# A two-layer diffusion backbone on one core: the partial-product stage put into a forced order of loads, with three modulation chunks moved

## The chip, the cores and the metric

The kernel runs on one core of one Trainium2 chip. The metric is the device time of one execution in microseconds (us). The engines are named as in the profile: PE (TensorE), PEld (its weight loads), DVE (VectorE), ACT (ScalarE), POOL (GpSimd) and SP (SyncE, which issues the DMA transfers here). L227 is line 227 of the kernel.

## What is computed

256 latent and 256 context tokens of width 2048 pass through two layers, all in fp32. Each layer has a token mixer (layer 0: pooling in four channel groups, layer 1: neighbourhood attention) and a gated MLP of width 5504 with a width-3 convolution. Shift, scale and gate of each sub-layer are made from the condition:

```
silu_c, silu_cc = jax.nn.silu(c), jax.nn.silu(c_ctx)
for i in range(DEPTH):
    ml = (silu_c @ w_mod[i] + b_mod[i]).reshape(B, 6, 1, D)
    mc = (silu_cc @ w_mod[i] + b_mod[i]).reshape(6, 1, 1, D)
    a_lat = modulate(rms_norm(h, norm1_g[i]), ml[:, 0], ml[:, 1])
    ...                                   # the mixer gives y_lat, y_ctx
    h = h + ml[:, 2] * y_lat
    h = h + ml[:, 5] * conv_ffn(modulate(rms_norm(h, norm2_g[i]), ml[:, 3], ml[:, 4]), ...)
    ...                                   # layer 0 does the same for the context stream
return rms_norm(h, final_norm_g)
```

## The kernel before

**Products.** A product in fp32 is made from three matmuls: high weight by high and by low input, low weight by high input. `load` (L145) fetches 128x1024 weights, 512 KB, with one transfer each, issued by SP (L150). `split` (L154) makes the high part with a CAST on ACT (L166) and the low part with a subtraction on DVE (L168). The loads land in six staging buffers (`rooms`, and for a time more that are lent). A load may start when the last reader of what lay in its buffer is done.

**Modulation.** Layer 0 needs 24 chunks of 512 columns of `w_mod`. `mod_pe` (L216) makes a chunk from eight loads in four pieces (0 to 3), directly from fp32, with no split: 16 matmuls for two pieces (L227), or 8 for each piece from chunk 21 on; an eviction on ACT (L243, `modev`); four transposes on PE (L248, `modt`); and a short finish on DVE. The chunks are made in a fixed order, by channel group g: chunks g, 4+g, 8+g, 16+g, 12+g; the gates 20 to 23 are last. `need(n)` drives this generator to the n-th piece.

**The partial stage** (up to about 425 us) handles the four channel groups g one after the other. `mixer(g)` (L539) pools the group: matmuls `pm` (L556 to 558), an evacuation `pz` on ACT (L613), and then the inputs of the MLP, `Ad` (high part on ACT L625, low part on DVE L626). Group 0 is worked with nothing else to do beside it; the list STEPS0 says how many pieces of modulation are called between its parts. `partial(g)` (L636) multiplies the `Ad` of this group with the gate and up columns of the first NS = 8 tiles of the MLP (`cg`, `cu`, L672 to 674, weights `wcg`, `wcu`). Between its 32 half steps the function `between` calls the next pieces of modulation by a due time (LEAD, RATE, PMAX), so that chunk 23 is complete before the stage is. Then `gu0(8)` makes the first full MLP tile (`g_8`, `u_8`, L761 to 763), for which a last correction `late` (L448) has to be in place, and `down0(0)` (L773) begins the down product (`d_0_0_0`, weights `wd_0_0`).

**The layer boundary.** The last down chunk is done by token stream, latent first (L782 to 810). Each result is added to `hl` or `hc` on DVE (L798). POOL adds up squares for the next norm (`n3q`, L328 and L340), PE reduces them over the partitions (`n3s`, L348), and layer 1 starts with the weights `wv_0` (CAST on ACT, low parts on DVE L168), used at L882.

**What sets the order.** A tile scheduler orders the instructions of each engine when the program is built. `high_priority` and `issue_after(x)` push it: the second says that an instruction stands behind x on its engine or waits for it. The loads of the partial stage have no such rule here: the scheduler has issued them partly in another order than the code has them.

Of the kernel before, what the change touches and what calls it, by code (L numbers as in the profile page):

```python
# [10 lines left out]
F32 = mybir.dt.float32  # L11
# [24 lines left out]
PMAX = 30  # L36

# [7 lines left out]
    ("g1_0", 2 * KT), ("g1_1", 2 * KT), ("g2_0", 2 * KT), ("g2_1", 2 * KT),  # L45
    ("bm_0", 6 * 2 * KT), ("bm_1", 6 * 2 * KT),
    ("pb", 2 * KT), ("ps", 2 * KT), ("fg", KT),
# [8 lines left out]
NVEC = _n  # L56


@with_exitstack
def kernel(ctx: ExitStack, tc: tile.TileContext, xT, cxT, wmod, wg, wu, wd, wp,  # L60
# [21 lines left out]

    vt = main.tile([P, NVEC], F32, name="vt")
    nc.sync.dma_start(vt, vec)

    def V(name):
        a, b = _OFF[name]
        return vt[:, a:b]
# [53 lines left out]
    fetched = []  # L142

    def load(src, cols, name):

        ts = []
        for j in range(0, cols, 1024):
            n = min(1024, cols - j)
            t = stage(f"{name}_{j}")
            fetched.append(nc.sync.dma_start(t[:, :n], src(j, j + n)).ins)  # L150
            ts.append((t, n))
        return ts

    def split(ts, name, share=0, keep=False):  # L154

        parts = []
        for j, (t, n) in enumerate(ts):
# [5 lines left out]
            with ExitStack() as behind:  # L163
                for ins in hold:
                    behind.enter_context(tc.issue_after(ins))
                nc.scalar.copy(hi[:, :n], t[:, :n])  # L166
# [11 lines left out]
    modT = {}  # L178

# [18 lines left out]
    def finish_mod(l, ch, streams, src):  # L198
# [9 lines left out]
        for b, v in enumerate(src):  # L208
            own = slice(32 * b, 32 * b + 32) if len(src) > 1 else slice(0, P)
            nc.vector.tensor_tensor(mt[own, :, 0:n], v, bias[own], op=ALU.add)  # L210
        if which in (1, 4):
            nc.vector.scalar_tensor_tensor(mt[:, :, 0:n], mt[:, :, 0:n], 1.0, dup(f"g{1 if which == 1 else 2}_{l}", 8 * q),
                                           op0=ALU.add, op1=ALU.mult)
        modT[l, ch] = mt

    def mod_pe(l, ch, sc, pool):  # L216
# [3 lines left out]
        for g in range(4):  # L220
            ts = load(lambda a, b: wmod[l, ch, g, :, a:b], 2048, f"wm{l}_{ch}_{g}")
            held.append((g, ts, fetched[-2:]))
            if ch > 20 or g % 2:
                with ExitStack() as behind:
                    for n, (gg, tt, _) in enumerate(held[::-1]):
# [14 lines left out]
            if g == 3:  # L240
                ev = pool.tile([P, 512], F32, tag="t2", name=f"modev{l}_{ch}")
                with tc.high_priority():
                    nc.scalar.copy(ev, ps)  # L243
            yield
        with tc.high_priority():
# [170 lines left out]
    with ExitStack() as ph0:  # L416
# [22 lines left out]
        def late(f):  # L439

            res = []
            for q in range(2):
# [36 lines left out]
        with ExitStack() as phs:  # L479
# [57 lines left out]
            STEPS0 = (9, 9, 11, 13, 15, 15, 15, 15)  # L537

            def mixer(g):  # L539
# [12 lines left out]
                def pointwise(ps, i, m):  # L552
# [5 lines left out]
                    nc.tensor.matmul(ps, lo[:, c : c + P], rh, start=False, stop=(i == 3))  # L558

                for i in range(4):  # L560
# [32 lines left out]
                    if g == 0:  # L593
                        for m in range(4):
                            pointwise(pms[m], i, m)
# [25 lines left out]
                for i in range(4):  # L621
                    k = 4 * g + i
                    a = ap0.tile([P, 2, 2, T], F32R, tag=f"A{k}", name=f"Ad{k}")
                    for s in both:
                        nc.scalar.activation(a[:, 0, s, :], h_of(s)[:, k, :], AF.Copy, scale=M(0, 4, k, s))  # L625
                        nc.vector.scalar_tensor_tensor(a[:, 1, s, :], h_of(s)[:, k, :], M(0, 4, k, s),  # L626
                                                       a[:, 0, s, :].bitcast(F32), op0=ALU.mult, op1=ALU.subtract)
# [3 lines left out]
                if g == 0:  # L631
                    for k in range(4):
# [871 lines left out]
```

## Time and profile before

| what | value |
|---|---|
| time, median of 3 runs | 3042.73 us (3042.56 to 3043.87) |
| time of the profiled execution | 3042.06 us |
| its span in the profile | 3040.3 us |
| busy share PE / PEld / DVE / ACT / POOL | 98% / 80% / 64% / 45% / 27% |
| bytes read from HBM | 557.03 MB |

The page gives each engine's busy time and cuts the span into 40 slices of 76 us. All slices but the first have PE busy to 90% or more; the first has 50% to 60%. The granted clock is in its top tenth in every slice, which hides stretches of a few microseconds; those are found with the windows view, which gives busy time, granted clock (PEclk), DMA share and GB/s for a stretch of one's choice. The waits view lists, for each engine, the line that waited, the instruction that released it, the total, the count and the longest wait. In the timeline, instructions of one line that follow each other are one row (x16 is 16 of them); the bracket at the row's end gives the idle time ahead of it and what ended it. A row of an SP issue shows when the transfer was given to the queue, and not when it lands.

### The profile page before, as it was taken

To read this page: it belongs to the slowest core of one execution; us is meant where nothing else is said; L and a number is where in the kernel's file an instruction comes from. 1 tells how busy PE (TensorE), PEld (TensorE's weight loads), DVE (VectorE), ACT (ScalarE), POOL (GpSimd) and SP (SyncE) were. 2 spreads that over 40 slices of the span, in tenths; PEclk is the share of its full clock that TensorE was granted. 3 is DMA by queue.
4 is the path that set the end of the run, shared out by engine and by line. 5 is a ranking of instruction groups with operands and counts; after the bars stand their busy time and mean duration, and the time that the engine had idled before them with its cause. 6 is when DMAs were issued, how large, how long until landed. Compare 5 with 4: busy or idle time off the path is not lost.

```text
span 3040.3 us, 41042 instructions
## 1 busy us (share of the span) xinstructions
PE 2974.5 (98%) x15128; PEld 2417.6 (80%) x15128; DVE 1941.3 (64%) x2782; ACT 1379.0 (45%) x2237; POOL 834.5 (27%) x820
## 2 busy tenths in 40 slices
PE   5999999999999999999999999999999999999998
PEld 2666668888888888888888888878888888888887
DVE  4455764386584857758485657474778666666666
ACT  4333454323333242433334534343556666666665
POOL 0000213303123030311315002020002566566665
PEclk9999999999999999999999999999999999999999
DMA  9888653384665747566482333333356555555563
GB/s 393 330 291 324 232 201 103 108 252 146 208 193 173 239 144 234 160 200 213 148 257 76 118 105 118 114 120 107 104 161 195 188 190 192 189 185 185 184 195 116
DMA packets 178791, 561.80 MB, mean 185 GB/s; under 512 B 17696, under 2 KB 22432, under 8 KB 178592
## 3 DMA queue, kind: packets, MB, share of 16 engines
q1 hardware_dynamic: 178592, 559.19, 56.4%
q8 instruction: 119, 1.95, 0.3%
q14 instruction: 80, 0.66, 0.1%
HBM read 557.03 MB, written 2.10 MB: 184 GB/s over the span
## 4 chain that ended last, share of the span: by engine, by line
PE 82%; issue 6%; POOL 1%; DVE 1%; ACT 1%; DMA 1%; SPq 0%; DVEq 0%; POOLq 0%; ACTq 0%
PE d L819 5%; PE d L820 5%; PE d L821 5%; PE u L1025 5%; PE g L1025 5%; PE d L1078 4%; PE g L761 4%; PE g L763 4%; PE g L762 4%; PE u L763 4%; PE u L761 4%; PE u L762 4%; PE u L1028 3%; PE g L1028 3%; PE d L1082 2%
## 5 line engine op out<-in xcount | busy, mean ns | idle before, releaser
L832 POOL TENSOR_TENSOR hl<-hl,dy 128x256 f32<-128x256 f32 x160 | 146.1, 913 | 942.2 <-ACT dy L831 942.0
L1094 POOL TENSOR_TENSOR hl<-hl,dy 128x256 f32<-128x256 f32 x320 | 332.1, 1074 | 188.3 <-ACT dy L1092 186.0
L286 DVE SCALAR_TENSOR_TENSOR macc<-wm,sc,macc 128x512 f32<-128x512 f32 (+1 forms) x360 | 328.9, 944 | 68.9 <-DMA wm<-wmod 67.6
L831 ACT ACTIVATE dy<-d,modT 128x256 f32<-128x256 f32 x320 | 133.1, 469 | 187.7 <-PE d L821 169.3
L832 POOL TENSOR_TENSOR hc<-hc,dy 128x256 f32<-128x256 f32 x160 | 129.3, 808 | 0.0
L168 DVE TENSOR_TENSOR wd_2l<-wd,wd_2h 128x1024 fp32r<-128x1024 f32 (+1 forms) x44 | 55.7, 1271 | 108.2 <-ACT wd_2h L166 107.0
L1092 ACT ACTIVATE dy<-d,modT 128x512 f32<-128x512 f32 x160 | 104.5, 684 | 43.0 <-PE d L1082 41.5
L1180 POOL TENSOR_TENSOR rk<-rk,rp 128x256 f32<-128x256 f32 x16 | 14.8, 926 | 324.0 <-DVE rk L1179 225.5
L227 PE MATMUL mod<-wm,sc 128*32 128x512 f32 x768 | 97.3, 622 | 5.9 <-DMA wm<-wmod 5.7
L168 DVE TENSOR_TENSOR wd_3l<-wd,wd_3h 128x1024 fp32r<-128x1024 f32 (+1 forms) x44 | 53.4, 1234 | 77.4 <-ACT wd_3h L166 76.0
L168 DVE TENSOR_TENSOR wd_1l<-wd,wd_1h 128x1024 fp32r<-128x1024 f32 (+1 forms) x44 | 53.7, 1224 | 61.2 <-ACT wd_1h L166 61.2
L615 POOL TENSOR_TENSOR hl<-hl,pz 128x256 f32<-128x256 f32 x12 | 11.8, 979 | 289.4 <-ACT pz L613 289.4
L166 ACT CAST wd_1h<-wd 128x1024 fp32r<-128x1024 f32 (+1 forms) x44 | 45.3, 1032 | 81.9 <-PE u L762 57.3
L168 DVE TENSOR_TENSOR wd_0l<-wd,wd_0h 128x1024 fp32r<-128x1024 f32 (+1 forms) x44 | 54.6, 1247 | 36.0 <-ACT wd_0h L166 35.9
L1269 ACT ACTIVATE sb<-sb,nm 128x512 f32<-128x512 f32 x64 | 46.2, 723 | 58.9 <-DVE nm L1265 57.4
L166 ACT CAST wd_0h<-wd 128x1024 fp32r<-128x1024 f32 (+1 forms) x44 | 45.3, 1033 | 54.9 <-PE u L1025 29.1
L1057 DVE TENSOR_TENSOR actb<-sgb,actb 128x256 fp32r<-128x256 f32 x43 | 50.8, 1181 | 25.9 <-ACT actb L1056 25.9
L819 PE MATMUL d<-act,wd_2h 128*128 128x512 f32 x172 | 67.1, 390 | 0.0
L820 PE MATMUL d<-act,wd_2h 128*128 128x512 f32 x172 | 66.9, 389 | 0.0
L821 PE MATMUL d<-act,wd_2l 128*128 128x512 f32 x172 | 66.9, 389 | 0.0
L821 PE MATMUL d<-act,wd_0l 128*128 128x512 f32 x172 | 66.9, 389 | 0.0
L819 PE MATMUL d<-act,wd_1h 128*128 128x512 f32 x172 | 66.9, 389 | 0.0
(1770 smaller groups left out, 9271.3 us busy)
## 6 DMA issues: line engine op xcount, KB each, us to landing
wm<-wmod SPq DMA_DIRECT2D x384, 512.0 KB, 6.1
wd<-wd SPq DMA_DIRECT2D x168, 512.0 KB, 4.4
wg<-wg SPq DMA_DIRECT2D x156, 512.0 KB, 4.7
wu<-wu SPq DMA_DIRECT2D x156, 512.0 KB, 4.6
wv<-wv SPq DMA_DIRECT2D x32, 512.0 KB, 3.8
wk<-wq SPq DMA_DIRECT2D x32, 512.0 KB, 3.9
wq<-wq SPq DMA_DIRECT2D x32, 512.0 KB, 3.8
wo<-wo SPq DMA_DIRECT2D x32, 512.0 KB, 4.6
```

What stands on the lines that cost most here:

```text
L168: eng.tensor_tensor(lo[:, :n], t[:, :n], hi[:, :n].bitcast(F32), op=ALU.subtract)
L286: nc.vector.scalar_tensor_tensor(acc[s], v, sc2[:, k, s : s + 1], acc[s], op0=ALU.mult, op1=ALU.add)
L761: nc.tensor.matmul(ps, hi[:, c : c + P], xh, start=(k == 0), stop=False)
L762: nc.tensor.matmul(ps, hi[:, c : c + P], xl, start=False, stop=False)
L763: nc.tensor.matmul(ps, lo[:, c : c + P], xh, start=False, stop=(k == KT - 1))
L819: nc.tensor.matmul(ps, hi[:, o : o + P], xh, start=(i == 0), stop=False)
L820: nc.tensor.matmul(ps, hi[:, o : o + P], xl, start=False, stop=False)
L821: nc.tensor.matmul(ps, lo[:, o : o + P], xh, start=False, stop=(i == n - 1))
L832: nc.gpsimd.tensor_tensor(h_of(s)[:, k, :], h_of(s)[:, k, :], y[:, s], op=ALU.add)
L1025: nc.tensor.matmul(ps, hi[:, c : c + P], flat(B[k]), start=(k == 0), stop=False)
L1028: nc.tensor.matmul(ps[:, T:], lo[:, c : c + P], B[k][:, 0], start=False, stop=(k == KT - 1))
L1094: nc.gpsimd.tensor_tensor(hl[:, k, :], hl[:, k, :], y[:, q], op=ALU.add)
```

## The change

It has six parts.

1. The table of vectors `vt` is loaded as two tiles. The first 320 columns (of layer 0) come first, as before; the other 616 are loaded behind chunk 12's first loads.
2. `in_turn`: from the start of the partial stage on, each load is issued after the load ahead of it in the code. This ends in `down0(0)`.
3. STEPS0 and `behind_of`: pieces of chunk 16 stand behind the pooling's pointwise matmuls. The eviction `modev` has no high priority any more. The first gate columns `wcg_0` are loaded ahead of chunk 12; of their two casts the first is held behind chunk 16's eviction and finish, and the second behind the second `Ad`. The first sums of the second norm stand behind that cast.
4. The due times are capped at LAST = 88. What is left of chunk 21 (its transposes) and chunks 22 and 23 are called from `gu0(8)`, after every eighth k (`one_more`), and from `down0(0)` (`late_mods`).
5. In the last group chunk 21's pieces are due earlier, and the first half of `late` for the first full tile is called at half step 24.
6. In the last down chunk the split of `wv_0` is held behind the fourth `hl` addition.

```
+LAST = 88
...
+    vt = [main.tile([P, n], F32, name=f"vt{i}") for i, n in enumerate((NFIRST, NVEC - NFIRST))]
+    nc.sync.dma_start(vt[0], vec[:, :NFIRST])
...
+            with ExitStack() as behind:
+                for ins in fetched[-1:] if in_turn else ():
+                    behind.enter_context(tc.issue_after(ins))
+                fetched.append(nc.sync.dma_start(t[:, :n], src(j, j + n)).ins)
...
                 with ExitStack() as behind:
+                    for x in behind_of:
+                        behind.enter_context(tc.issue_after(x))
...
-                with tc.high_priority():
-                    nc.scalar.copy(ev, ps)
+                EVICT[l, ch] = nc.scalar.copy(ev, ps).ins
...
-            STEPS0 = (9, 9, 11, 13, 15, 15, 15, 15)
+            STEPS0 = (9, 9, 9, 10, 13, 13, 15, 15)
...
+                        if i > 1:
+                            behind_of[:] = [ins]
...
+                        ts = FIRST.pop() if FIRST else columns(g, nm, wsrc, fa)
+                        if g == fa == q == 0:
+                            hold[:] = [EVICT[0, 16], FINISH[0, 16]]
+                            parts = split(ts[:1], f"wc{nm}{g}_{fa}", keep=True)
+                            hold[:] = second
+                            parts += split(ts[1:], f"wc{nm}{g}_{fa}b", keep=True)
...
-                    need(min(20 * g + LEAD + RATE * (half + 1) // 32, 20 * g + LEAD + PMAX))
+                    need(min(20 * g + LEAD + RATE * (half + 1) // 32, 20 * g + LEAD + PMAX, LAST))
...
+                        need(20 * g + 21)
...
+                    if g == 3 and half == 24:
+                        EARLY[NC] = late(NC, (0,))[0]
...
-            need(97)
-            nbank[0] = 0
+            need(LAST)
...
+                    if k % 8 == 7 and aside is not None:
+                        aside(ins)
...
+                            if not s and m == 3:
+                                hold[:] = [res.ins]
...
+        def one_more(ins):
+            behind_of[:] = [ins]
+            need(done[0] + 1)
+            behind_of.clear()
...
+        def late_mods(mg, m, ins):
+            if mg < 2 and m % 2:
+                one_more(ins)
+            if mg == 2 and m == 0:
+                need(97)
+                in_turn.clear()
+                nbank[0] = 0
```

The built program has two PE rows more (13927 for 13925), four DVE rows and two ACT rows fewer, one SP row more, and the same POOL rows. The order on PE, ACT and SP differs only in the partial stage and the first full tile; behind that only DVE differs, at the layer boundary.

**Place 1, the end of pooling in group 0, on ACT.** Before, these rows run from the eviction of chunk 8 to the first `Ad`. `ph` are the pooled inputs, `pz` the evacuated pooling results, `n2q` squares for the second norm:

```order
L243 COPY modev_8_400<-mod_8_307 128x512
L590 CAST ph_422<-pf_420 128x512
L590 CAST ph_460<-pf_458 128x512
L243 COPY modev_16_487<-mod_16_410 128x512
...
L613 ACTIVATE pz_520<-pm_3_343,gbi_331,gsc_330 128x256 x2
L166 CAST wcg_0h_565<-wcg_0_0_561 128x1024
L166 CAST wcg_0h_569<-wcg_0_1024_563 128x1024
L322 ACTIVATE n2q_545<-hl 128x256
L322 ACTIVATE n2q_545<-hc 128x256
L322 ACTIVATE n2q_549<-hl 128x256
L625 ACTIVATE Ad_525<-hl,modT_16_494 128x256
```

And in the changed program:

```order
L609 CAST ph_396<-pf_394 128x512
L256 COPY modev_8_423<-mod_8_308 128x512
L609 CAST ph_432<-pf_430 128x512
L634 ACTIVATE pz_478<-pm_0_341,gbi_332,gsc_331 128x256 x2
...
L634 ACTIVATE pz_493<-pm_3_344,gbi_332,gsc_331 128x256 x2
L256 COPY modev_16_510<-mod_16_455 128x512
L173 CAST wcg_0h_551<-wcg_0_0_512 128x1024
L646 ACTIVATE Ad_530<-hl,modT_16_521 128x256
L646 ACTIVATE Ad_530<-hc,modT_16_521 128x256
```

The eviction of chunk 16 has moved from ahead of the eight `pz` to behind them. One cast of `wcg_0` and the three squares no longer stand ahead of the first `Ad`. (The `pz` of the pooling tiles between the first and the last are left out of these rows.)

**Place 2, the end of the first full tile, on PE and on SP.** In the changed program these are the PE rows from the end of `g_8` to the first down product; pieces 1 to 3 of chunk 22 stand among the last matmuls of `u_8`:

```order
L241 MATMUL mod_22_3548<-wm_22_1_1024_3583,sc 32x512 x2
L241 MATMUL mod_22_3548<-wm_22_1_0_3581,sc 32x512 x2
L241 MATMUL mod_22_3548<-wm_22_2_1024_3628,sc 32x512 x2
L241 MATMUL mod_22_3548<-wm_22_2_0_3626,sc 32x512 x2
L804 MATMUL u_8_3601<-A_0_3_3487,wu_8h_3597 128x512
L805 MATMUL u_8_3601<-A_0_3_3487,wu_8l_3598 128x512
L803 MATMUL u_8_3601<-A_0_3_3495,wu_8h_3597 128x512
L804 MATMUL u_8_3601<-A_0_3_3495,wu_8h_3597 128x512
L805 MATMUL u_8_3601<-A_0_3_3495,wu_8l_3598 128x512
L241 MATMUL mod_22_3548<-wm_22_3_1024_3660,sc 32x512 x2
L241 MATMUL mod_22_3548<-wm_22_3_0_3658,sc 32x512 x2
L868 MATMUL d_0_0_0_3680<-act_3201,wd_0_0h_3672 128x512
```

The loads for them on SP, in the changed program, with the semaphores that each waits for:

```order
L155 DMA wu_8_0_3589<-wu 128x1024 [waits DMAHW7_49,DVE_49]
L155 DMA wu_8_1024_3591<-wu 128x1024 [waits DMAHW0_49,DVE_49]
L155 DMA wm_22_2_0_3626<-wmod 128x1024 [waits DMAHW1_49,PE_49]
L155 DMA wm_22_2_1024_3628<-wmod 128x1024 [waits DMAHW2_49]
L155 DMA wm_22_3_0_3658<-wmod 128x1024 [waits DMAHW3_49,PE_49]
L155 DMA wm_22_3_1024_3660<-wmod 128x1024 [waits DMAHW4_49]
L155 DMA wd_0_0_0_3668<-wd 128x1024 [waits DMAHW5_49]
L155 DMA wd_0_0_1024_3670<-wd 128x1024 [waits DMAHW6_49,DVE_49]
```

And the same place on SP before:

```order
L150 DMA wm_23_3_0_3488<-wmod 128x1024 [waits DMAHW7_49,DVE_49,PE_49]
L150 DMA wm_23_3_1024_3490<-wmod 128x1024 [waits DMAHW6_49,DVE_49,PE_49]
L150 DMA wg_8_0_3595<-wg 128x1024 [waits DMAHW0_49,PE_49]
L264 DMA wm_0_0_4857<-wmod 128x1024 [waits DMAHW1_49,PE_49]
L150 DMA wu_8_0_3656<-wu 128x1024 [waits DMAHW2_49,PE_49]
L150 DMA wg_8_1024_3597<-wg 128x1024 [waits DMAHW3_49,PE_49]
L150 DMA wu_8_1024_3658<-wu 128x1024 [waits DMAHW6_49,DVE_49]
...
L150 DMA wd_0_0_1024_3719<-wd 128x1024 [waits DMAHW0_49,DVE_49]
L150 DMA wd_0_0_0_3717<-wd 128x1024 [waits DMAHW1_49,DVE_49]
```

Before, chunk 23's loads were issued ahead of the full tile's. Now chunk 22's stand among them, in the order of the code. The PE wait of `wm_22_3_0` is for the last matmul that reads `wm_22_1_0`, the second of the PE rows above: the load goes into that buffer. The loads of `wd_0_0` stand behind it on SP. (Rows of chunk 0 of layer 1, L264, are left out between the last ones.)

**Place 3, the layer boundary, on DVE.** Before, in the last down chunk (`d_10_3`):

```order
L798 SCALAR_TENSOR_TENSOR hl<-d_10_3_0_0_12936,modT_23_3515,hl 128x256
...
L168 TENSOR_TENSOR wv_0l_13077<-wv_0_0_13072,wv_0h_13076 128x1024
L798 SCALAR_TENSOR_TENSOR hl<-d_10_3_1_0_12950,modT_23_3515,hl 128x256
L168 TENSOR_TENSOR wv_0l_13081<-wv_0_1024_13074,wv_0h_13080 128x1024
L798 SCALAR_TENSOR_TENSOR hl<-d_10_3_2_0_12964,modT_23_3515,hl 128x256
L798 SCALAR_TENSOR_TENSOR hl<-d_10_3_3_0_12978,modT_23_3515,hl 128x256
```

And in the changed program:

```order
L843 SCALAR_TENSOR_TENSOR hl<-d_10_3_0_0_12938,modT_23_3928,hl 128x256
...
L843 SCALAR_TENSOR_TENSOR hl<-d_10_3_1_0_12952,modT_23_3928,hl 128x256
L843 SCALAR_TENSOR_TENSOR hl<-d_10_3_2_0_12966,modT_23_3928,hl 128x256
L843 SCALAR_TENSOR_TENSOR hl<-d_10_3_3_0_12980,modT_23_3928,hl 128x256
L175 TENSOR_TENSOR wv_0l_13079<-wv_0_0_13074,wv_0h_13078 128x1024
L175 TENSOR_TENSOR wv_0l_13083<-wv_0_1024_13076,wv_0h_13082 128x1024
```

The two low parts have moved behind the four additions.

More of the change, by code (lines that the diff above doesn't have):

```diff
@@ L437, with late @@
         wsh = main.tile([P, 2, NS, 2], F32, name="wsh")
-        def late(f):
-            res = []
-            for q in range(2):
+        EARLY = {}
+        def late(f, qs=(0, 1)):
+            res = [EARLY.pop(f)] if f in EARLY else []
+            for q in qs[len(res) :]:
                 if f < NC:
@@ L849 @@
             more()
-        down0(0, chunks[0], [acts[f] for f in chunks[0]], more)
+        def late_mods(mg, m, ins):
[5 more added lines that the diff above has]
+                nbank[0] = 0
+                rooms[:] = [r for r in rooms if -r not in ring]
+        down0(0, chunks[0], [acts[f] for f in chunks[0]], more, late_mods)
         while rest:
```

83 lines of the change are left out of this document (52 added, 31 removed).

## The prediction, made before the changed kernel had run

> **What bounds the kernel now.** I read the page's busy times first, then the waits of PE, then windows around each wait.
>
> ```profile
> PE 2974.5 (98%) x15128; PEld 2417.6 (80%) x15128; DVE 1941.3 (64%) x2782; ACT 1379.0 (45%) x2237; POOL 834.5 (27%) x820
> ```
>
> PE is busy 98% of the span and PE's work is unchanged, so the change can only move PE's idle time and the time at a lowered clock. The waits of PE, as line, releaser, total us, count and longest:
>
> ```profile
> PE cg L672 <- ACT Ad L625: 7.1, 4, 4.5
> PE mod L227 <- DMA wm<-wmod: 5.7, 3, 2.8
> PE modt L248 <- ACT modev L243: 4.2, 5, 1.2
> PE n3s L348 <- POOL n3q L340: 2.5, 1, 2.5
> PE g L761 <- DVE late L448: 2.4, 1, 2.4
> PE cu L672 <- ACT wcu_4h L166: 2.2, 1, 2.2
> ```
>
> The six sum to 24 us in all, and the edits aim at these waits. What a wait costs beyond itself is in the windows (stretch and its length, PE busy, granted clock, DMA share, GB/s):
>
> ```profile
> 50.00:75.00 25.00, 19.09 (x117) 1.00 1.03 417
> 75.90:79.30 3.40, 3.00 (x8) 0.50 1.03 408
> 396.80:400.20 3.40, 3.34 (x12) 0.50 0.38 151
> 419.50:424.20 4.70, 4.70 (x13) 0.64 0.71 235
> 450.00:1600.00 1150.00, 1150.00 (x5095) 1.00 0.59 184
> 1656.30:1663.10 6.80, 6.52 (x31) 0.50 0.15 57
> ```
>
> Between 450 and 1600 us PE has no idle time at all, so nothing is won there. Behind four waits (those of 4.5, 2.2, 2.4 and 2.5 us) PE ran at about half clock for a while: 3.4 us at 0.50 is worth 1.7 us, 4.7 us at 0.64 also 1.7, 6.8 us at 0.50 worth 3.4. A wait of 2.3 us can thus cost 4. From 50 to 75 us the DMA share is full at 417 GB/s, so there the loads set the pace: 512 KB in 1.25 us.
>
> [...]
>
> **Start (parts 1 to 3): 4.2 us gained.** PE and ACT before:
>
> ```profile
> 54.51 1.92 PE L227 MATMUL mod<-wm,sc 128*32 128x512 f32 x16
> 57.17 0.66 PE L248 MATMUL modt<-ident,modev 128*128 128x128 f32 x4 [0.73 <-ACT modev L243]
> 65.32 1.92 PE L227 MATMUL mod<-wm,sc 128*32 128x512 f32 x16
> 67.97 0.66 PE L248 MATMUL modt<-ident,modev 128*128 128x128 f32 x4 [0.73 <-ACT modev L243]
> 68.81 1.92 PE L227 MATMUL mod<-wm,sc 128*32 128x512 f32 x16 [0.18 <-PE modt L248]
> 75.22 0.73 PE L672 MATMUL cg<-Ad,wcg_0h 128*128 128x512 f32 x2 [4.49 <-ACT Ad L625]
> ```
>
> ```profile
> 57.01 1.14 ACT L590 CAST ph<-pf 128x512 fp32r<-128x512 f32 x2
> 67.34 0.58 ACT L243 COPY modev<-mod 128x512 f32<-128x512 f32 x1 [9.19 <-PE mod L227]
> 67.82 3.76 ACT L613 ACTIVATE pz<-pm,gbi,gsc 128x256 f32<-128x256 f32 x8
> 71.42 2.04 ACT L166 CAST wcg_0h<-wcg 128x1024 fp32r<-128x1024 f32 x2
> 74.23 0.54 ACT L625 ACTIVATE Ad<-hl,modT 128x256 fp32r<-128x256 f32 x1
> ```
>
> ```profile
> 68.76 0.18 DVE L250 TENSOR_REDUCE modT<-modt 128x8 f32<-128x32 f32 x1
> ...
> 69.67 0.16 DVE L212 SCALAR_TENSOR_TENSOR modT<-modT,vt 128x8 f32<-128x8 f32 x1
> ```
>
> Before, `modt` of chunk 16 was over at 68.63, yet the first `Ad` began at 74.23: eight `pz` (3.76) and two casts (2.04) stood ahead of it on ACT. In the changed program:
> - `vt` is 616 x 4 x 128 bytes = 315 KB shorter at the front; at 417 GB/s the loads run 0.75 us earlier.
> - The last `ph` cast stands behind chunk 8's eviction. PE then waits for eviction and cast: 0.58 + 0.57 + 0.2 of hand-over = about 1.4 us, in place of the 0.73 at 57.17.
> - PE's work up to chunk 16's last matmul is the same, which thus ends at 67.24 - 0.75 + 1.4 - 0.73 = 67.1.
> - The pooling matmuls now end ahead of chunk 16 (both halves, 2 x 1.9 us), at about 63.3. The `pz` run beside chunk 16, until 63.3 + 0.8 + 3.8 = 67.9. The eviction stands behind them: 0.58, to 68.4; `modt` 0.66, to 69.05; chunk 16's finish on DVE, which took 1.1 from 68.76 to 69.83 between additions, 0.7 by my estimate with fewer of them; then the first `Ad`, and `cg` starts 1.0 us after it (74.23 to 75.22): **70.75**, 4.47 us earlier.
> - The 1.92 us of chunk 12 that stood ahead of `cg` (68.81) now stand behind it: -1.92.
> - The idle time ahead of `cg` falls from 4.49 to about 1.7 us, so the half clock of 75.9 to 79.3 goes: +1.70.
>
> Sum: 4.47 - 1.92 + 1.70 = **4.2 us gained**. Bounds: 1 lost (loads bind again and a half clock returns) to 6 gained (the two new idles of 1.4 vanish too).
>
> **Middle (part 2, groups 1 to 3): 0.** Loads in the order of the code can wait for buffers that the scheduler's order had avoided. I counted, for each load, the PE work between the matmul that frees its buffer and the matmul that uses it. Of all of them the tightest are the eight loads of chunk 20's second half, which one matmul lets go: the last lands 4.1 + 7 x 1.25 = 12.9 us after it (4.1 us for a lone load, below) and is used 13.6 us after it. That is cover of 0.7 us. Bounds: 0.5 gained, 3 lost.
>
> **End of the stage (parts 4 and 5): 8.0 gained, 6.4 lost.** What goes: the waits of 2.23 (`wcu_4` is no longer issued late, between chunk 23's loads) and 2.36 us (`late` is made early), and the half clock behind each, 1.7 and 1.7: **8.0**. What is moved, the matmuls of chunks 22 and 23, costs PE the same at the new place. But place 2 shows a new wait. These rows carry it:
>
> ```profile
> 391.67 0.39 PE L672 MATMUL cg<-Ad,wcg_4h 128*128 128x512 f32 x1
> ...
> 392.13 0.39 PE L674 MATMUL cg<-Ad,wcg_4l 128*128 128x512 f32 x1
> 392.44 1.06 PE L227 MATMUL mod<-wm,sc 128*32 128x512 f32 x8
> 393.44 0.50 PE L674 MATMUL cg<-Ad,wcg_4l 128*128 128x512 f32 x1
> ```
>
> ```profile
> 413.69 0.33 SPq L150 DMA_DIRECT2D wu<-wu  x1
> ```
>
> ```profile
> 417.78 1.04 ACT L166 CAST wu_8h<-wu 128x1024 fp32r<-128x1024 f32 x1 [0.85 <-DMA wu<-wu]
> ```
>
> ```profile
> 412.44 1.23 DVE L168 TENSOR_TENSOR wg_8l<-wg,wg_8h 128x1024 fp32r<-128x1024 f32 x1 [3.21 <-ACT wg_8h L166]
> ```
>
> A wide matmul takes 0.23 us (two from 391.67 to 392.13), a piece of modulation 1.0 (392.44 to 393.44), a lone load 4.1 from issue to its cast (413.69 to 417.78). `wm_22_3_0` can be issued only when piece 1 of chunk 22 is done. `wm_22_3_1024`, the first that PE reads, lands 4.1 + 1.25 = 5.4 us after that. Until then PE has one piece and five matmuls: 1.0 + 5 x 0.23 = 2.15. It waits **3.3 us**. Then piece 3 runs to 6.4. The loads of `wd_0_0`, queued behind on SP, land at 6.7 and 8.0; cast 1.04: `d_0_0_0` starts at 7.9 and its third matmul, which needs the low part (1.2), at 9.1. Without waits that would be at 2.15 + 1.0 + 0.46 = 3.6. So 5.5 us late; 0.4 for the second load's low part and 0.5 for some half clock: **6.4 lost**. Bounds of this loss: 0 (the pieces of chunk 22 run earlier beside `g_8` than their places say) and 8.5 (a full 3.4 us more at half clock, +1.7, and DVE late). Net 1.6 gained; bounds 8 gained, 1 lost (0 when the first waits return in part).
>
> **Layer boundary (part 6): 0.4 lost.**
>
> ```profile
> 1652.13 2.21 DVE L168 TENSOR_TENSOR wv_0l<-wv,wv_0h 128x1024 fp32r<-128x1024 f32 x1
> ```
>
> ```profile
> 1651.97 1.29 POOL L328 TENSOR_TENSOR n3q<-n3q,n3q 128x512 f32<-128x512 f32 x1 [1.28 <-ACT n3q L322]
> 1653.34 1.59 POOL L340 TENSOR_TENSOR n3q<-n3q,n3q 128x256 f32<-128x256 f32 x1
> ```
>
> ```profile
> 1655.00 1.52 POOL L340 TENSOR_TENSOR n3q<-n3q,n3q 128x256 f32<-128x256 f32 x2
> ```
>
> ```profile
> 1656.58 1.87 PE L348 MATMUL n3s<-ones,n3q 128*128 128x1 f32 x8 [2.51 <-POOL n3q L340]
> ```
>
> The low part begun at 1652.13 took 2.21 us for 1.23, beside a POOL addition begun earlier; then the POOL addition of 1653.34 took 1.59 for 0.76 (half of 1.52), until the low part was over. So one excludes the other, and who began first holds. Now both low parts fall where POOL's three additions are. First addition 1653.34 to 1654.1, low part to 1655.2, second to 1655.9, low part again, third to 1656.95: `n3s` 0.4 later. Bounds: 1.1 lost; 4.4 gained, if the additions pass undisturbed (below).
>
> [...]
>
> **Sum**: 3042.06 of the profiled execution - 4.2 - 0 - 1.6 + 0.4 = 3036.7; that execution lies 0.67 under the median of the runs, so I give **3037.4 us**, 0.18% under 3042.73.
>
> **Rivals.**
> 1. *Chunk 22 brings no wait.* For it: only place and semaphore speak for the wait, no trace. Against: 5.4 us of landing with 2.15 of cover. Then 6.4 less: **3031**.
> 2. *POOL's additions pass.* If all three additions begin ahead of the low parts, `n3s` starts at about 1655.7, the wait falls to 1.6 us and the 3.4 us of half clock may go: 4.4 + 0.4 less: **3032.6**. Against: DVE's queue has nothing between the fourth `hl` and the low parts.
> 3. *The start gains nothing:* the three idles of 1.4, 1.4 and 1.7 us in 12 us, new between 58 and 71, lower the clock for 6.8 us (as after 1656) and cost 3.4: **3040.8**. For it: the idle of 2.23 was enough.
> 4. *Slower: one late buffer holds all loads.* SP issues in order, so a load that waits for a buffer now holds the loads behind it. If landing behind chunk 20's release takes over 13.6 us in place of 12.9, PE waits. Each of the four pieces can then be 1.3 to 2.7 late, plus 1.7 of half clock: about 4 us a time. If all groups (1 to 3) have such a place, 3 x 4 = 12 and the end loses its 8.5 in place of 6.4: 3037.4 + 14 = **3051**. Against it: the counts above leave cover, if a thin one.
>
> **How the numbers follow.** A run can tell about 0.2% (6.1 us) from no change: faster is below 3036.6, slower above 3048.8. Chances: forecast 0.45, own range 3034 to 3041; rival 1 0.17, rival 2 0.13, rival 3 0.12, rival 4 0.13. Faster: rivals 1 and 2, and the lower third of the forecast: 0.17 + 0.12 + 0.15 = 0.44. Slower: the larger part of rival 4, 0.10. Same: 0.46. The range, 3029 to 3047, takes in rivals 1 to 3 and the milder half of rival 4.
>
> **What would show it.** Start: `cg` of group 0 at about 70.8 us, its wait 1.7, clock 1.00 from 75 to 80. Middle: the first mark behind it keeps its lead of 4 us to 380 us; a wait of `mod` for `wm` of over 1 us would be rival 4. End: no wait of `cu` for `wcu_4h` and of `g` for `late`; a wait of `mod` for `wm` of 3.3 and of `d` for `wd_0h` of about 1.5. Boundary: a POOL addition of L340 stretched over 1.5 us, `n3s` waiting about 2.9. I'm wrong if the wait of chunk 22 isn't there, or if the lead of the start is lost ahead of 380 us.

## The result: slower by 0.18%, where 0.18% faster was forecast

The changed kernel took 3047.10 us (median of 20 runs, 3044.50 to 3049.75), the kernel before 3041.55 (20 runs, 3038.82 to 3044.72). The ratio is 1.0018, with a 95% interval of 1.0011 to 1.0025. The forecast was 3037.4 us, and the range ended at 3047.0. The profiled execution of the changed kernel took 3045.37 us with a span of 3043.6, against 3042.06 and 3040.3.

**The profile after.** PE's busy time is the same as before to 1.4 us:

```profile
PE 2973.1 (98%) x15128; PEld 2415.3 (79%) x15128; DVE 1947.1 (64%) x2782; ACT 1380.5 (45%) x2237; POOL 834.8 (27%) x820
```

So what was lost is idle time and clock. The waits of PE, in the same columns as before:

```profile
PE mod L241 <- DMA wm<-wmod: 13.5, 4, 4.6
PE modt L263 <- ACT modev L256: 6.1, 5, 2.1
PE cg L706 <- ACT Ad L646: 4.1, 2, 2.5
PE n3s L363 <- POOL n3q L355: 3.4, 1, 3.4
PE d L868 <- ACT wd_0h L173: 1.6, 1, 1.6
...
PE g L803 <- DVE late L465: 0.9, 1, 0.9
...
PE cu L708 <- DVE wcu_4l L175: 0.7, 1, 0.7
```

`cg` fell from 7.1 to 4.1, and the waits of `cu` for `wcu_4h` (2.2) and `g` for `late` (2.4) are gone or down to 0.9. But the modulation's matmuls now wait 13.5 us for their weights, where it was 5.7, and the longest single wait is 4.6. Of the 13.5 us, 5.4 stand at 36 and 44 us, about as before (5.5); the waits of 4.6 and 3.5 are new. I put both traces side by side by matmuls that exist in both. The start times in us:

| matmul | before | after | after minus before |
|---|---|---|---|
| first of the first norm, `n1s` | 21.63 | 19.99 | -1.64 |
| first transpose of `ptu`, group 0 | 114.25 | 108.35 | -5.90 |
| first low `pm` of group 2 | 233.01 | 228.02 | -4.99 |
| last `n2s` on the squares | 342.34 | 337.84 | -4.50 |
| last low `cu` on `wcu_0` | 374.93 | 376.47 | +1.54 |
| first `d` on `wd_3h` | 475.67 | 479.92 | +4.25 |
| last `d` on `wd_3h`, layer boundary | 1663.97 | 1667.65 | +3.68 |
| first `n5s`, end | 3027.34 | 3030.60 | +3.26 |

At 114 us the lead is larger than the 4.2 us forecast for the start. Two places take it back: 6.0 us between 342 and 375 and 2.7 between 375 and 476. From there to the end almost nothing changes. (Between the marks from 342 to 476 both traces have the same number of modulation matmuls, 56 and 72, so that moved pieces don't blur these two figures. Chunk 23 is made behind the full tile: the order on PE and SP thus changes in the first down product too.)

**First place: chunk 20's second half.** PE in the changed kernel, and before:

```profile
339.29 1.92 PE L241 MATMUL mod<-wm,sc 128*32 128x512 f32 x16
345.82 3.64 PE L241 MATMUL mod<-wm,sc 128*32 128x512 f32 x16 [4.61 <-DMA wm<-wmod]
```

```profile
344.01 1.92 PE L227 MATMUL mod<-wm,sc 128*32 128x512 f32 x16
347.00 1.92 PE L227 MATMUL mod<-wm,sc 128*32 128x512 f32 x16
```

The 16 matmuls wait 4.61 us and then take 3.64 instead of 1.92, at half clock (0.50 from 344.95 to 351.77). The loads, as SP issued them, after and before:

```profile
328.92 2.66 SPq L155 DMA_DIRECT2D wm<-wmod  x4
331.62 2.73 SPq L155 DMA_DIRECT2D wcu<-wu  x2
334.45 14.15 SPq L155 DMA_DIRECT2D wm<-wmod  x8
```

```profile
317.11 2.79 SPq L150 DMA_DIRECT2D wm<-wmod  x6
324.36 1.06 SPq L150 DMA_DIRECT2D wcu<-wu  x2
333.28 2.52 SPq L150 DMA_DIRECT2D wm<-wmod  x4
```

The loads behind one matmul are eight: six of chunk 20 (pieces 1 to 3) and the two of `wcu_0` between them, and not eight of chunk 20's second half, as the prediction has it; a half has four. Before, two of these six were among the loads that began at 317, the two of `wcu_0` went at 324, and only four waited for matmuls, two at 333 and two at 335. In the forced order all eight wait for one matmul (at 328.92; everything is 4 to 5 us earlier here). The windows of the changed kernel (stretch, its length, PE busy, granted clock, DMA share, GB/s):

```profile
50.00:75.00 25.00, 20.51 (x124) 1.00 1.03 418
75.00:85.00 10.00, 9.24 (x57) 1.00 1.02 379
330.00:337.00 7.00, 7.00 (x49) 1.00 0.76 218
340.00:355.00 15.00, 10.26 (x46) 0.77 0.81 308
420.00:445.00 25.00, 19.80 (x88) 0.86 0.54 205
```

From 330 to 337 the transfers moved 218 GB/s instead of the 418 of the stage's start. The last of the eight landed at 345.73, 16.8 us after the release; I had worked out 12.9. The difference is not spread over the eight. The DMA view gives the time from issue to landing, here for the loads issued at 328.92 and 329.29:

```profile
wm<-wmod SPq DMA_DIRECT2D x1, 512.0 KB, 4.0
wm<-wmod SPq DMA_DIRECT2D x1, 512.0 KB, 8.7
```

So the first landed at 332.9 and the second at 338.0, 5.1 us behind it. The other six then landed 1.2 to 1.4 us apart, as counted.

**Second place: the first full tile**, PE in the changed kernel:

```profile
435.88 1.07 PE L241 MATMUL mod<-wm,sc 128*32 128x512 f32 x8 [3.52 <-DMA wm<-wmod]
438.58 0.80 PE L868 MATMUL d<-act,wd_0h 128*128 128x512 f32 x1 [1.64 <-ACT wd_0h L173]
439.18 0.63 PE L869 MATMUL d<-act,wd_0h 128*128 128x512 f32 x1
...
443.42 0.63 PE L869 MATMUL d<-act,wd_0h 128*128 128x512 f32 x1
```

These are the two waits that the prediction named, of 3.52 and 1.64 us where it had 3.3 and 1.5. The matmuls behind them are of 0.63 us, not 0.39: the granted clock is 0.50 from 437.1 to 443.9.

**The boundary**, POOL, DVE and PE in the changed kernel:

```profile
1657.59 4.06 POOL L355 TENSOR_TENSOR n3q<-n3q,n3q 128x256 f32<-128x256 f32 x3
```

```profile
1657.69 3.39 DVE L175 TENSOR_TENSOR wv_0l<-wv,wv_0h 128x1024 fp32r<-128x1024 f32 x2
```

```profile
1661.71 1.18 PE L363 MATMUL n3s<-ones,n3q 128*128 128x1 f32 x8 [3.38 <-POOL n3q L355]
```

The three additions took 4.06 us in a row (before, two undisturbed ones took 1.52), and two low parts 3.39 (before, an undisturbed one 1.23). `n3s` waits 3.38 instead of 2.51. One by one, the additions took 0.74, 1.58 and 1.59 us and the low parts 1.72 and 1.74: each but the first began beside the other engine's instruction and ended 0.6 to 1.1 us after that one was over (an addition at 1658.33, a low part at 1659.41, an addition at 1659.99, a low part at 1661.08, an addition at 1661.65). This is the exclusion that the prediction drew from the rows of before.

### The profile page after: what moved, and what is told of

Read it like the earlier page. It is cut to its first block, busy times and chain, and to the rows that moved or that the text cites. A ratio compares the mean times of both kernels' runs of the same rounds, so it can differ in the third digit from the quotient of the medians.

```text
span 3043.6 us, 40932 instructions
## 1 busy us (share of the span) xinstructions
PE 2973.1 (98%) x15128; PEld 2415.3 (79%) x15128; DVE 1947.1 (64%) x2782; ACT 1380.5 (45%) x2237; POOL 834.8 (27%) x820
## 3 DMA queue, kind: packets, MB, share of 16 engines
q8 instruction: 119, 1.95, 0.3%
## 4 chain that ended last, share of the span: by engine, by line
PE 87%; issue 7%; DMA 2%; DVE 2%; POOL 1%; ACT 1%; SPq 0%; DVEq 0%; POOLq 0%; ACTq 0%
PE d L868 5%; PE d L870 5%; PE d L869 5%; PE u L1088 5%; PE g L1088 5%; PE d L1141 4%; PE u L803 4%; PE u L804 4%; PE u L805 4%; PE g L803 4%; PE g L805 4%; PE g L804 4%; PE u L1091 3%; PE g L1091 3%; PE d L1145 2%
## 5 line engine op out<-in xcount | busy, mean ns | idle before, releaser
L880 ACT ACTIVATE dy<-d,modT 128x256 f32<-128x256 f32 x320 | 133.7, 470 | 193.0 <-PE d L870 173.5
L241 PE MATMUL mod<-wm,sc 128*32 128x512 f32 x768 | 97.9, 627 | 13.5 <-DMA wm<-wmod 13.5
L868 PE MATMUL d<-act,wd_0h 128*128 128x512 f32 x172 | 68.3, 397 | 1.6 <-ACT wd_0h L173 1.6
L241 PEld LDWEIGHTS mod<-wm,sc 128*32 128x32 f32 x768 | 21.4, 112 | 58.7 <-issue 56.5
L869 PE MATMUL d<-act,wd_0h 128*128 128x512 f32 x172 | 67.9, 395 | 0.0
```

The costliest lines, as they stand in the source:

```text
L868: nc.tensor.matmul(ps, hi[:, o : o + P], xh, start=(i == 0), stop=False)
L869: nc.tensor.matmul(ps, hi[:, o : o + P], xl, start=False, stop=False)
```

## The experiments

Theory A: the time is lost where a forced order holds a run of loads behind one buffer, once at chunk 20 and once at chunk 22 in the full tile. The rivals are named in the expectations. All edits are to the changed kernel. The table has the median of each and its ratio to the kernel before on the same chip. The last column is the stretch from the last `n2s` to the first `d` on `wd_3h` in its trace, which holds both places (133.3 us before, 142.1 in the changed kernel). Each of the last four rows is one step away from "both, without part 6", which itself was measured on another chip than they were.

| kernel | median us | ratio (95%) | stretch us |
|---|---|---|---|
| the change again | 3048.58 | 1.0020 (1.0011 to 1.0029) | 141.4 |
| chunk 20 freed | 3040.28 | 0.9994 (0.9985 to 1.0003) | 134.9 |
| all chunks in the stage | 3039.98 | 0.9995 (0.9986 to 1.0004) | 133.7 |
| both | 3036.05 | 0.9980 (0.9970 to 0.9991) | 130.4 |
| only chunk 22 in the stage | 3038.62 | 0.9990 (0.9981 to 0.9999) | 132.3 |
| without part 6 | 3044.64 | 1.0005 (0.9996 to 1.0014) | 142.3 |
| without part 1 | 3045.61 | 1.0012 (1.0003 to 1.0020) | 134.0 |
| both, without part 6 | 3036.31 | 0.9982 (0.9974 to 0.9991) | 128.8 |
| ... and without part 3 | 3035.01 | 0.9975 (0.9965 to 0.9985) | 126.6 |
| ... and without part 1 | 3036.97 | 0.9977 (0.9968 to 0.9986) | 130.4 |
| ... with chunk 23 in the down product | 3034.38 | 0.9971 (0.9961 to 0.9981) | 127.5 |
| ... and forced order in the start alone | 3032.93 | 0.9968 (0.9956 to 0.9979) | 131.2 |

**Chunk 20's loads freed.** The loads of chunk 20 and the first up columns of the last group get no place in the order:

```
-                for ins in fetched[-1:] if in_turn else ():
+                for ins in fetched[-1:] if in_turn and not name.startswith(("wm0_20", "wcu3_0")) else ():
```

> All of the change, but chunk 20's loads and wcu_0's of the last group are free of the forced order. Theory A (the forced order holds eight loads behind one buffer): the two loads of wcu_0 and two of chunk 20 go ahead again, the 4.6 us wait of mod for wm at 345.8 us and the half clock behind it are gone, 5.5 us less than the changed kernel: about 3041.6 us, ratio to before 1.000. Rival B (transfers happened to be slow between 331 and 337 us in that one execution, 125 to 250 GB/s): the order is not the cause, 0 to 1.5 us less, about 3046.

The wait is gone. PE in this kernel, in the place of the two rows above:

```profile
342.84 3.64 PE L241 MATMUL mod<-wm,sc 128*32 128x512 f32 x32
```

All 32 matmuls run in one go at full clock (1.00 from 340 to 355 us; 3.64 us for 32, which the changed kernel needed for 16). The stretch from the last `n2s` to the last low `cu` on `wcu_0`, 32.6 us before, is 31.8 here and 36.2 to 38.6 in the changed kernel, its repeat and the three variants below that keep chunk 20 in the order and part 1. The ratio falls from 1.0018 or 1.0020 to 0.9994, some 7 us, a little more than expected. The scheduler also put the first half's matmuls later, so that it is the loads' order with what it does to PE's order that was changed here.

**All chunks inside the stage**, with the early half of `late` kept:

```
-LAST = 88
+LAST = 97
...
-            need(LAST)
+            need(97)
+            in_turn.clear()
+            nbank[0] = 0
...
+        rooms[:] = [r for r in rooms if -r not in ring]
...
-        res = gu0(NS, one_more)
+        res = gu0(NS)
...
-        down0(0, chunks[0], [acts[f] for f in chunks[0]], more, late_mods)
+        down0(0, chunks[0], [acts[f] for f in chunks[0]], more)
```

> All of the change, but chunks 21 to 23 are made inside the partial stage as before (the early late half is kept). Theory A (chunk 22 in the full tile costs 5.3 us of waits and some half clock): these go; the waits before, of wcu_4 and late, don't come back, since the loads are in the code's order and late is early: 3 to 4 us less than the changed kernel, about 3043.6, ratio 1.0007. Rival C (the move was needed: in the forced order the loads of wcu_4 and wg_8 stand behind chunk 23's, and PE waits for them as long): no gain, about 3047. The wait of 4 to 5 us for chunk 20 stays by A, and is under 1.5 us by B (slow transfers by chance).

The ratio fell by as much, to 0.9995, about 7 us and more than expected; rival C (no gain) is out. In its place the waits at the end are 1.0 us for `wg_8h` and 0.5 for `wg_8l`. Chunk 20's wait stayed, at 3.98 us, and so rival B (chance) is out too:

```profile
345.86 3.22 PE L241 MATMUL mod<-wm,sc 128*32 128x512 f32 x16 [3.98 <-issue]
```

**Both edits together.**

> Both edits together. Theory A: the two losses stand in different places and add: 9 us less than the changed kernel, about 3038 us, ratio to before 0.9988. By B 3043, by C 3041.6.

0.9980, as theory A had it (0.9988 was expected, inside the interval). The stretch falls from 142.1 to 134.9 or 133.7 by one edit and to 130.4 by both. The two places are separate losses, though the single effects sum to somewhat more than the common one: 7.2 and 8.4 by the trace against 11.7.

**Without part 6.** The two lines that set `hold` in the last down chunk are taken out.

> All of the change without part 6 (the low parts of wv_0 among the additions, as before). The boundary took 32.2 us in the changed kernel and 32.8 before (first to last mark there), so I expect 0.6 us more than the changed kernel, 3047.7, with the half clock of 6.8 us from 1660 us on back; rival: no difference in the boundary beyond the phase of the clock, 3047.1. By A the wait for chunk 20 at about 345 us is again 4 to 5 us; by B (chance) it is under 1.5.

```profile
1661.05 1.05 PE L363 MATMUL n3s<-ones,n3q 128*128 128x1 f32 x8 [2.52 <-POOL n3q L355]
```

The wait of `n3s` is 2.52 again. It is 2.51 or 2.52 in each of the seven profiles without part 6, the one of before among them, and 3.38 to 3.40 in each of the seven with it. So part 6 adds 0.9 us of waiting: shown. The expected 0.6 us slower did not come; what the time makes of it, see below. Chunk 20's wait was 4 to 5 us again.

**The change again**, beside the next three.

> The changed kernel again, so that it stands beside the other edits on one chip. Ratio to before 1.0005 to 1.0018. The wait for chunk 20's second half is again 4 to 5 us at about 345 us, the transfers ahead of it slow (150 to 260 GB/s) from 331 to 337 us.

```profile
339.50 1.92 PE L241 MATMUL mod<-wm,sc 128*32 128x512 f32 x16
345.12 3.50 PE L241 MATMUL mod<-wm,sc 128*32 128x512 f32 x16 [3.70 <-issue]
```

The wait stands at the same place with 3.70 us, a little under the 4 to 5 expected; the row names "issue" where it was a load that landed at its end. The time is that of the first result.

**Only chunk 22 in the stage**; chunk 23 stays in the down product:

```
-LAST = 88
+LAST = 92
...
-        res = gu0(NS, one_more)
+        res = gu0(NS)
```

> All of the change, but chunk 22 stays in the partial stage; only chunk 23 is made in the first down product. Theory A (the loss at the end is chunk 22's loads, held behind one buffer in the full tile, and nothing else of the move): the waits of 3.3 and 1.6 us and their half clock go, chunk 23 costs nothing where it is: 4 to 5 us less than the changed kernel, as much as with the whole move undone (0.9995 there). Rival D: each piece between the down products costs by itself, or their loads hold wd_0 up: half of that or less.

0.9990 beside 1.0020 of the changed kernel on the same chip: 9 to 10 us, more than the 4 to 5 expected, and no less than with the whole move undone. `d` waits 0.46 us where it waited 1.64, and `mod` not at all:

```profile
431.56 0.50 PE L868 MATMUL d<-act,wd_0h 128*128 128x512 f32 x1 [0.46 <-ACT wd_0h L173]
```

Chunk 22 in the full tile is the loss; chunk 23 in the down product shows no cost beside intervals of 0.1% to either side. Rival D is out.

**Without part 1.** The second part of the vectors is loaded right behind the first:

```
     nc.sync.dma_start(vt[0], vec[:, :NFIRST])
+    nc.sync.dma_start(vt[1], vec[:, NFIRST:])
...
-            with tc.issue_after(fetched[-1]):
-                nc.sync.dma_start(vt[1], vec[:, NFIRST:])
```

> All of the change without part 1: the second part of the vectors is loaded right behind the first. The first norm's matmuls stood at 21.63 us before and at 19.8 to 20.6 in the five changed kernels so far. My sum had 0.75 us for the 315 KB at 417 GB/s. Expected: those matmuls at 21.2 to 21.7 (1.3 us for the 315 KB, since transfers are slower at the start), and the total 0.75 to 1.5 us over the changed kernel. Rival E: the loads ahead are not what sets the first norm, the mark stays at 20 and the total is the same.

```profile
21.07 3.12 PE L384 MATMUL n1s<-ones,n1q 128*128 128x1 f32 x14 [21.07 <-DVE n1q L344]
```

The first norm came about 1.1 us later, as expected, but the kernel was not slower (1.0012 beside 1.0020, with intervals that overlap). Neither theory had that. In its profile the wait at chunk 20 was shorter than elsewhere:

```profile
345.59 1.92 PE L242 MATMUL mod<-wm,sc 128*32 128x512 f32 x16 [1.71 <-issue]
```

PE came as long after the release as in the changed kernel (12.3 us), but the second of the eight loads landed 1.6 us behind the first in place of 5.1 (335.73 and 337.36), and the last 13.9 us after the release in place of 16.8. Why it was quicker in this execution, no run separates.

**Both edits and no part 6.**

> Chunk 20's loads and wcu_0 free of the forced order, chunks 21 to 23 inside the stage, and no part 6. Theory A with part 6 as a loss: the wait of n3s falls from 3.4 to 2.5 us, 0.9 to 1.5 us less than the same without the last edit (ratio 0.998): 0.9976. Rival F: the boundary hangs on the phase of the clock alone: 0.998.

0.9982 beside 0.9980: no difference seen, but theory A's 0.9976 lies inside the interval too. With the run above (1.0005 beside 1.0018 and 1.0020 in other sessions) the two readings of part 6 disagree, so that its effect on the time is not settled; only its wait of 0.9 us is.

**Both, without part 6, and without part 3**: group 0's old order.

```
-                EVICT[l, ch] = nc.scalar.copy(ev, ps).ins
+                with tc.high_priority():
+                    EVICT[l, ch] = nc.scalar.copy(ev, ps).ins
...
-            STEPS0 = (9, 9, 9, 10, 13, 13, 15, 15)
+            STEPS0 = (9, 9, 11, 13, 15, 15, 15, 15)
...
-                        if i > 1:
-                            behind_of[:] = [ins]
...
+                if g == 0:
+                    for k in range(4):
+                        n2.add(h_of, k)
...
-                        if g == fa == q == 0:
+                        if False:
...
-                if i == 6:
-                    need(n + 1)
-                    FIRST.append(columns(0, "g", wg, 0))
```

> The version without the two waits and without part 6 (ratio 0.9982, 5.5 us under before), now also without part 3: group 0's old order of pooling, modulation and casts. My sum had 4.2 us of the start, 0.75 of them from the shorter vector load and the rest from part 3. Theory G: part 3 carries what gain is left: the wait of cg for Ad is 4.5 us again and half clock behind it, 3 to 4 us slower, ratio 0.9993. Rival H: most is from the shorter load and the order of the loads; the same 0.9982.

The wait of `cg` is 3.57 us and half clock follows (0.86 from 75 to 85 us, where it is 1.00 in the changed kernel), as theory G said:

```profile
73.30 0.73 PE L708 MATMUL cg<-Ad,wcg_0h 128*128 128x512 f32 x2 [3.57 <-ACT Ad L645]
```

But the kernel is not slower: 0.9975 with an interval up to 0.9985. Theory G falls. One trace of each does not say where the gain of part 3 goes. Beside the changed kernel this one is 3.0 us behind at the transpose of `ptu` (111.34 and 108.35) and level at the first low `pm` of group 2 (228.17 and 228.02): in group 1 the changed kernel waits once more for the first `Ad` and has half clock behind it (160.63 to 164.04 us), where this one waits 1.13 us and has none. The changed kernel:

```profile
158.84 0.73 PE L706 MATMUL cg<-Ad,wcg_0h 128*128 128x512 f32 x2 [2.48 <-ACT Ad L646]
```

But by the last `n2s` it is 5.0 us behind again (342.80 and 337.84). Beside the profile of "both, without part 6" it is 0.3 behind, 3.4 ahead and 1.6 behind at these three marks; that profile had half clock in the start, at 68.8 to 75.6 us.

**Both, without part 6, and without part 1.**

> The version without the two waits and without part 6, now also without part 1. The first norm stood 1.1 us later without part 1 in the run before, yet that kernel was not slower (1.0012 beside 1.0020). Theory I: the 1.1 us are lost here, since no wait behind swallows them: ratio 0.9985 to 0.9987. Rival J: the 316 KB are paid wherever they stand, as the transfers are full up to 75 us, and a half clock can go either way: 0.9982 or less.

0.9977: no loss seen, as rival J had it, though the interval just reaches theory I's 0.9985. Part 1 brings the first norm forward by 1.1 to 1.6 us, and no run shows anything of it in the time.

**Both, without part 6, with chunk 23 in the down product.**

> Without the wait for chunk 20 and without part 6; of part 4, chunk 22 stays in the partial stage and chunk 23 is made in the first down product. Theory A: chunk 23 in the down product costs nothing and takes a little from the end of the stage: 0.998 or up to 1.5 us better than the version with all chunks in the stage, 0.9977. Rival D: its pieces cost by themselves: 0.9985.

0.9971, the better side of theory A's range; the intervals of this and the one with all chunks in the stage overlap.

**The forced order in the start alone.** All chunks in the stage, no part 6, and `in_turn` cleared once group 0 is pooled:

```
             behind_of.clear()
+            in_turn.clear()
             with tc.issue_after(fetched[-1]):
```

> The version with all chunks in the stage and without part 6, with the loads in forced order only up to the end of group 0's pooling; all later ones as the scheduler has them. Theory K: what the forced order gave beyond the start is the issue of wcu_4 ahead of chunk 23's loads, whose wait cost 2.2 us and 1.7 of half clock: 3 to 4 us slower, 0.9993. Rival L: the forced order gives nothing behind the start: 0.9982.

0.9968, the lowest ratio of all, about 10 us under the kernel before. Theory K (the order is needed for `wcu_4`) falls, and rival L's 0.9982 lies above the interval too. `cu` waits 1.95 us for `wcu_4` again, but no half clock follows (the `cu` matmuls behind the first are of 0.39 to 0.40 us, like the `cg` ones ahead of the wait).

```profile
391.42 0.50 PE L706 MATMUL cu<-Ad,wcu_4h 128*128 128x512 f32 x1 [1.95 <-ACT wcu_4h L173]
```

That no half clock follows is luck in part: see rival 3 below. In group 1 `cg` waits 1.01 us for `Ad`, as before the change, and not about 2.5 as with the order kept, and no half clock follows there; the first low `pm` of group 2 is at 225.84, 2.2 us ahead of the changed kernel. By this one trace the forced order costs something in group 1 too.

## Why the prediction was wrong, point by point

**Start, 4.2 us gained: the rows came as forecast, the gain at the end is not shown.** `cg` began at 70.04 us (70.75 forecast), with a wait of 1.62 and no half clock:

```profile
67.76 0.66 PE L263 MATMUL modt<-ident,modev 128*128 128x128 f32 x4 [1.64 <-ACT modev L256]
70.04 0.73 PE L706 MATMUL cg<-Ad,wcg_0h 128*128 128x512 f32 x2 [1.62 <-ACT Ad L646]
```

The first norm came 1.6 us earlier, not 0.75; by the two pairs with and without part 1 the shorter vector load is worth 1.1 to 1.6. The 315 KB were priced at 417 GB/s, but up to 14 us the transfers moved 284 to 293. At 114 us the lead was 5.9, and 5.0 at 233. About 1.0 of it is likely chance: the half clock ahead of the stage, from 38 us on, lasted 10.24 us before and 6.83 after, and 3.41 in another variant. What failed is that a lead at a mark was taken for a gain at the end: the versions without part 3 and without part 1 show no loss.

**Middle, 0: this step failed.** The prediction counted chunk 20's loads as the tightest, with 0.7 us of cover, and set the cost to 0. Both sides of that count were off. PE came 12.3 us after the release (345.82 - 4.61 - 328.92), not 13.6, and the last load landed after 16.8, not 12.9. The spacing of 1.25 us held for all but one: what the count lacks is the 5.1 us between the first landing and the second. So 0.7 of cover became 4.5 of waiting, and half clock came on top. Without the late landing, in the profile without part 1, PE still waited 1.71 us. That was rival 4, with a chance of 0.13. Its mechanism, its place and its price for one place (about 4 us; 3.6 to 6.0 in the five traces with the order and part 1) held; that it would strike at three places did not. The lead was lost ahead of 380 us, which the prediction had named as a sign of being wrong.

**End, 8.0 gained and 6.4 lost: the waits were right, the balance was not.** The new waits were foreseen to 0.2 us. The half clock behind them had been set at 0.5 us. It lasted 6.8 us, 5.3 of them with PE busy, which is worth 2.7; in the other variants with chunk 22 in the full tile it lasted from 3.4 to 10.2. The gain of 8.0 was too large as well: the waits that go leave smaller ones in their place, 0.9 for `late` and 0.7 for the low part of `wcu_4`. So 1.6 gained became 2.7 lost; these terms make 1.4 of it (3.5 + 1.6 + 2.7 + 0.9 + 0.7 - 8.0), and the rest is not accounted for. The runs say the same: chunk 22 out of the full tile alone is worth 0.3%. Rival 1 (no such wait) is out, by the row of 3.52.

**Boundary, 0.4 lost: right in mechanism, `n3s` waited 0.9 longer, not 0.4.** The prediction's sequence ends the third addition at 1656.95, which leaves it no time behind the second low part; added up with its own steps (1.1 and 0.7) it ends at 1657.7, about 1.2 later than before. The additions took 4.06 us, and POOL and DVE took turns in the order in which the instructions began (1657.59, 1657.69, 1658.41, 1659.33 and 1660.07); rival 2 (the additions pass) is out. That the boundary as a whole came out 0.6 us shorter in the trace is a matter of the clock, in the changed kernel 0.76 over 7 us, or 1.7 us, where it was 0.50 over 6.8 us, or 3.4. It can't be put down to part 6: the half clock there lasts 3.4 us in some profiles and 6.8 in others, with part 6 and without.

```profile
1661.00:1668.00 7.00, 6.29 (x39) 0.76 0.43 142
```

**Rival 3, half clock in the start.** In the changed kernel's profile it did not come. In that of the kernel with chunk 20 freed, whose instructions up to there are the same, it lasted from 70.15 to 76.97 us, and the transpose of `ptu` was at 112.15 and not at 108.35. So rival 3's mechanism and its price (3.4 us) held, in some executions. First the changed kernel, then the other; the idles of 1.64 and 1.62 us stand in the first two rows, and in both rows of the other:

```profile
65.05:68.47 3.42, 1.72 (x16) 1.00 1.04 416
68.47:71.88 3.41, 1.84 (x14) 1.00 1.03 423
71.88:75.29 3.41, 3.41 (x20) 1.00 1.03 414
```

```profile
66.73:70.15 3.42, 1.09 (x10) 1.00 1.03 418
70.15:73.56 3.41, 2.48 (x10) 0.50 1.02 419
```

The stretches are chosen so because the clock changed only at such times here: in each of the 14 traces all changes of the clock ahead of the last one lie a multiple of 3.413 us apart (41.16, 47.99, 160.63, 164.04, 344.95, 351.77 and so on in the changed kernel; 38.39, 48.63, 75.93, 79.35, 164.68, 168.09 and so on before). In the first kernel the two idles of 1.64 and 1.62 us fall into two such stretches, 1.7 and 1.6 us idle. In the other, one stretch takes the whole of the first and 0.7 of the second, 2.3 us idle in all, and half clock follows. From 50 to 445 us this holds in all 14 traces: behind each of the 23 stretches at full clock with 1.87 us or more of idle time came half clock, behind none with less than 1.65, and behind some of those between. Of the 23, the trace of before has three (from 72.52, 393.37 and 417.27; 2.70, 2.15 and 2.23 us idle) and that of the changed kernel three (from 157.21, 341.53 and 433.69; 1.88, 3.41 and 2.35), each with half clock behind it; between the two bounds, 1.65 us (before, from 161.27) was followed by half clock, 1.69 (changed kernel) and 1.78 (before) by full. The 1.95 us of `cu` at 391.42 fell on two stretches, with 0.4 and 1.6 us.

**The sum.** -5.0 at 233 us, +0.5 to 342, +6.0, +2.7, -0.6 at the boundary and -0.4 behind it make, up to rounding, the 3.3 us by which the marks at the end differ, of two single executions; the medians of 20 differ by 5.55. A single execution can be off by the 3.4 us that 6.8 us of half clock are worth, as in the start above.

**What stays open.** Why the second load landed so late. Of the six profiles with chunk 20 in the forced order it came 3.2 to 5.1 us behind the first in five and 1.6 in the one without part 1, where PE waited 1.71 us and not 3.6 to 4.6. The forced order is not the cause: with chunk 20 freed, four loads start behind that pause in place of eight, the second is 2.8 to 5.6 us behind the first in six of seven profiles, and PE waits for none of the four. Where it was late, SP took 0.9 to 1.5 us to issue the second load (1.33 in the changed kernel), and 0.4 to 0.5 where it was not (0.38 before); which causes which, no run separates. Open too are where the gains of parts 1 and 3 go, and what part 6 costs in time.

## What to carry to other kernels

Forcing loads into program order made eight loads wait for one late buffer here, and PE waited 4.61 us for the last of them. Before doing it, list for each load the instruction that frees its buffer, the loads behind it, and the time until the last of them lands, as measured in such a burst (16.8 us here) and not worked out from the best rate (12.9). The counted cover of 0.7 us for eight transfers was a cost here, not a zero. And a lead at the start is only a gain if no later wait swallows it: the 4.5 us at 342 us were gone at 375. The version that kept the order only where the loads were the limit has the lowest ratio here, though its interval overlaps those of the three beside it. Before reading a difference of 2 to 4 us from single profiles, compare their half clocks: in the start, with the same instructions, 6.8 us of it, worth 3.4 us, stand in one execution and none in another.

## What was not expected of the hardware

Whether half clock followed an idle time of PE of 1.6 to 2.2 us went, in these traces, with how it lay between the times, multiples of 3.413 us apart, at which the clock changed; they differ between the two traces (38.39, 75.93 and 164.68 before, 41.16, 160.63 and 344.95 in the changed kernel): 1.95 us (`cu` at 391.42), split by it, was followed by full clock, 2.23 us before by half clock, and two idles of 1.6 us by either. And in a burst of 512 KB loads after a pause the second landed 5.1 us behind the first in the changed kernel, while those behind it came 1.2 to 1.4 us apart.
